# Hybrid attention trunk, one core: the sink column of the first attention, written by ScalarE instead of GpSimd

## The chip, the core and the metric

The kernel runs on one core of a Trainium2 chip. A core has five engines, each with its own in-order queue: TensorE (PE, with its weight loads shown apart as PEld), VectorE (DVE), ScalarE (ACT), GpSimd (POOL) and SyncE (SP), which here issues the DMAs. Engines wait for each other by semaphores; an instruction that waits holds up everything behind it on its own engine and nothing elsewhere. SBUF holds working tiles of 128 partitions, PSUM holds matmul results.

The metric is the device time of one launch in microseconds; lower is better. It is taken as a median of several runs.

## The reference

Two layers work on 1024 latent tokens and 256 context tokens, width 1024. Layer 0 uses windowed grouped-query attention with a sink logit per head, layer 1 a 2-D neighbourhood attention. The part that matters here is the softmax of layer 0, for the latent blocks and likewise for the context tokens:

```python
s_sink = jnp.broadcast_to(sink_l[None, :, :, None, None], s_lat.shape[:-1] + (1,))
p = jax.nn.softmax(jnp.concatenate([s_lat, s_ctx, s_sink], axis=-1), axis=-1)
p_lat = p[..., :span].astype(v.dtype)
p_ctx = p[..., span:span + C].astype(v.dtype)
```

The sink is one more logit in the sum of each row. Its probability is not used, only its share in the denominator.

## The kernel before

The program builds u (the modulated tokens, in two float32r parts, high and low, as everywhere for near-float32 matmuls), then the first attention, the output projection and layer norm of layer 0, the second attention, and the last projection with its layer norm. Names with `_A` belong to the first attention, with `_B` to the second.

The first attention is cut into 8 pairs of heads, 10 blocks of 128 queries (8 latent, 2 context) and 2 heads: 160 units, called softmaxes below. Each has a row of 640, 512 or 256 keys per query. A unit k passes through these steps:

- `qkA`: PE forms the scores S_A (L741 and L742) in PSUM.
- `sm_first`: DVE adds the mask, scales by -1/8 and takes the minimum of the row and of the negated sink in one instruction (L322), which writes s_A and, by an accumulator read, the minimum m_A. POOL copies the negated sink of the head (column of the tile `nsk`) into the column behind the row (L327). ACT takes exp(-s + m) over the row and that column and sums it into sum_A (L329, with an accumulator read).
- `sm_second`: DVE takes the reciprocal rs_A of the sum (L333), POOL scales the row by it (L334).
- `sm_transpose`: PE transposes the row by 128x128 pieces into PSUM (T_A, L341), ACT rounds it to the high part (pth_A, L345), DVE forms the low part (ptl_A, L347).
- `pvA_fn`: PE multiplies with the values (L770), ACT and DVE join the halves in `otmp` (L779, L781), POOL multiplies by the gate (L784).

s_A has three buffers, so unit k writes where unit k-3 stood; S_A and T_A share two PSUM buffers. The scores run three units ahead of the transposes.

Beside these steps PE does the projections of the gate and of the next pair's queries (pj, L212 to L214), whose weights ACT and POOL split into parts (wh L166, wl L168); the queries pass through the rotary product (L501 to L504, L696, L697). DVE, POOL and ACT also form the dot products of the layer's modulation from rows of a weight matrix loaded by DMA (gj L654, gw L655, L636), up to seven in each pair of heads.

The order on each engine is set by the framework's scheduler: it takes the program's instructions with priorities (the softmax's first part is lifted by `LIFT_A`, some others by `lift`), estimates when operands are ready, and emits one fixed queue for each engine. The proportion of projection pieces to attention steps is set by `merge`. So an edit of one instruction can move others.

Of the kernel before, what the change touches and what calls it, by code (L numbers as in the profile page):

```python
# [14 lines left out]
AF = mybir.ActivationFunctionType  # L15
# [69 lines left out]
def build(tc, i, out):  # L85
    nc = tc.nc
# [223 lines left out]
    def sm_first(pl, sc, width, bias, scale, init, name):  # L310

        s = Sub()
        s.w = width
        s.t = pl.tile([P, 641], F32, tag="s", bufs=3, name=f"s_{name}")
        s.m = pl.tile([P, 1], F32, tag="m", bufs=4, name=f"m_{name}")
        s.sum = pl.tile([P, 1], F32, tag="sum", bufs=4, name=f"sum_{name}")
        s.rs = pl.tile([P, 1], F32, tag="rs", bufs=4, name=f"rs_{name}")
        outp, in1 = s.t[:, :width], bias
        if len(bias.shape) == 3:
            outp = outp.rearrange("p (a b) -> p a b", a=bias.shape[1])  # L320
            sc = sc.rearrange("p (a b) -> p a b", a=bias.shape[1])
        nc.vector.tensor_tensor_reduce(  # L322
            outp, sc, in1, scale, init if init is not None else 3e38, ALU.add, ALU.min, accum_out=s.m
        )
        n = width
        if init is not None:
            nc.gpsimd.tensor_copy(s.t[:, width : width + 1], init)  # L327
            n += 1
        nc.scalar.activation(s.t[:, :n], s.t[:, :n], AF.Exp, bias=s.m, scale=-1.0, accum_out=s.sum)  # L329
        return s  # L330
# [400 lines left out]
    def qkA(k):  # L731
        p, b, h = subsA[k]
        q = qA[2 * p + h]
        sc = psbig(f"S_A{k}")
        ql = q[:, b * P : (b + 1) * P]
        n = len(tilesA(b)) * P - 256
        for l in range(2):
            kk = kA[p // 2, l]
            if n:
                t0 = tilesA(b)[0] * P  # L740
                mm(sc[:, 512 - n : 512], ql, kk[:, t0 : t0 + n], start=l == 0, stop=l == 1)  # L741
            mm(sc[:, 512:768], ql, kk[:, S:T], start=l == 0, stop=l == 1)  # L742
        if b == 0:
            m = msk[:, 128:640]
        elif b == 7:
            m = msk[:, 640:1152]
        elif b >= 8:
            m = msk[:, 384:640]
        else:
            m = msk[:, 0:640]  # L750
        hd = 2 * p + h
        with lift(LIFT_A):
            stA[k] = sm_first(px, sc[:, 512 - n : 768], n + 256, m, -0.125, nsk[:, hd : hd + 1], f"A{k}")
# [245 lines left out]
    bias = [bp.tile([P, 2, 640], F32, name=f"bias{n}") for n in range(2)]  # L999
# [67 lines left out]
    def qkB(k):  # L1067
        h, jp, r = subsB[k]
        j = 2 * jp + r
        sc = psbig(f"S_B{k}")  # L1070
        ql = qB[h][:, j * P : (j + 1) * P]
        t0, t1 = max(j - 1, 0) * P, min(j + 2, 8) * P
        n = t1 - t0

        ll, lc = (slice(512 - n, 512), slice(512, 768)) if j < 7 else (slice(512, 768), slice(256, 512))
        for l in range(2):
            kk = kB[h, l]
            mm(sc[:, ll], ql, kk[:, t0:t1], start=l == 0, stop=l == 1)
            mm(sc[:, lc], ql, kk[:, S:T], start=l == 0, stop=l == 1)  # L1079
        bt = bias[h % 2].rearrange("p x t -> p (x t)")  # L1080
        b0 = 0 if 0 < j < 7 else 768 if j == 0 else 384
        with lift(LIFT_B if k >= BARE_B else 0):
            stB[k] = sm_first(bp, sc[:, 512 - n : 768] if j < 7 else sc[:, 256:768], n + 256, bt[:, b0 : b0 + n + 256], -1.0, None, f"B{k}")
# [312 lines left out]
```

## Time and profile before

| what | value |
|---|---|
| median of 3 runs | 1434.78 us (1433.45 to 1435.99) |
| the profiled execution | 1434.58 us |
| its span, first to last instruction | 1432.8 us |
| first attention's softmaxes, first to last exponential | 102.9 to 572.4 us |
| ACT busy over the whole span | 51% |
| POOL busy over the whole span | 45% |

The span is what the profile's rows cover; 1.8 us of the execution lie around it. A row of grouped instructions reads: source line, engine, operation, output and input tiles with shapes, count, then busy time in us and mean duration in ns, then the idle time of the engine just before them and who ended it. A row of waits reads: who waits, for whom, us in total, times, longest. A row of the timeline reads: start, duration, engine, line, operation, and in brackets the idle time before it with its releaser.

### The profile page before, as it was taken

Reading aid. Unit: us, or ns where it says so; the run is one execution under the profiler, and the core shown is the slowest. Engines: PE = TensorE matmul, PEld = TensorE weight load, DVE = VectorE, ACT = ScalarE, POOL = GpSimd, SP = SyncE. Lnnn points to the kernel's source line nnn. Section 1 sums busy time; section 2 is a strip of 40 time slices with the busy share of each in tenths; the row PEclk is TensorE's granted clock in tenths of the full one; section 3 lists DMA queues with packets and bytes.
Section 4 is the critical chain, followed back from the end, with each engine's and each line's share of the span. In section 5 each row is a group of like instructions: output and inputs, shape, how many; then the busy total and the mean of one; then the engine's idle time right before and its main releaser. Section 6 shows DMA issues by size and latency. Waiting matters only on the chain. (4 is left out here: it accounts for less than half of the span.)

```text
span 1432.8 us, 25169 instructions
## 1 busy us (share of the span) xinstructions
PE 1390.7 (97%) x8816; PEld 1217.8 (85%) x8816; DVE 973.4 (68%) x2203; ACT 732.5 (51%) x1559; POOL 642.1 (45%) x790
## 2 busy tenths in 40 slices
PE   9999999999999999999999999999999999998996
PEld 6988898888888888888898899888988899887885
DVE  4658887878878788666433766565666565656598
ACT  4337776676776778332222545555455554557200
POOL 0326676667666666233301333333233333347583
PEclk9999999999999999999999999999999999999998
DMA  9472114123222124434287576465555564376653
GB/s 368 174 234 82 55 57 127 50 78 101 70 71 63 56 83 132 132 118 147 75 255 219 143 200 180 138 171 153 172 165 163 147 187 140 122 189 197 178 149 107
DMA packets 127597, 202.39 MB, mean 141 GB/s; under 512 B 9712, under 2 KB 65392, under 8 KB 127472
## 3 DMA queue, kind: packets, MB, share of 16 engines
q1 hardware_dynamic: 127472, 200.79, 46.6%
q8 instruction: 70, 1.15, 0.3%
q14 instruction: 55, 0.45, 0.1%
HBM read 145.18 MB, written 55.57 MB: 140 GB/s over the span
## 5 line engine op out<-in xcount | busy, mean ns | idle before, releaser
L334 POOL TENSOR_SCALAR s_B<-s_B,rs_B 128x640 f32<-128x640 f32 (+1 forms) x128 | 101.5, 793 | 285.2 <-DVE rs_B L333 249.5
L212 PE MATMUL pj<-uBh,wh 128*128 128x512 f32 (+1 forms) x448 | 175.8, 392 | 0.0
L213 PE MATMUL pj<-uBl,wh 128*128 128x512 f32 (+1 forms) x448 | 170.2, 380 | 0.0
L214 PE MATMUL pj<-uBh,wl 128*128 128x512 f32 (+1 forms) x448 | 170.0, 379 | 0.0
L329 ACT ACTIVATE s_B<-s_B,m_B 128x640 f32<-128x640 f32 (+1 forms) x128 | 102.9, 804 | 129.2 <-DVE m_B L322 129.1
L329 ACT ACTIVATE s_A<-s_A,m_A 128x641 f32<-128x641 f32 (+2 forms) x160 | 119.6, 748 | 82.8 <-DVE m_A L322 59.7
L168 POOL TENSOR_TENSOR wl<-wr,wh 128x512 fp32r<-128x512 f32 x64 | 87.0, 1360 | 162.9 <-ACT wh L166 150.0
L334 POOL TENSOR_SCALAR s_A<-s_A,rs_A 128x640 f32<-128x640 f32 (+2 forms) x160 | 129.4, 809 | 65.2 <-DVE rs_A L333 59.1
L322 DVE CUSTOM_DVE_ANT_0 s_A<-S_A,msk,nsk 128x640 f32<-128x640 f32 (+2 forms) x160 | 123.6, 774 | 32.3 <-PE S_A L742 17.2
L212 PE MATMUL pj<-uAh,wh 128*128 128x512 f32 (+1 forms) x384 | 140.1, 365 | 0.8 <-DVE otmp L781 0.8
L347 DVE TENSOR_TENSOR pt_B<-T_B,pt_B 128x640 fp32r<-128x640 f32 (+1 forms) x128 | 101.0, 789 | 55.3 <-ACT pt_B L345 54.8
L213 PE MATMUL pj<-uAl,wh 128*128 128x512 f32 (+1 forms) x384 | 137.6, 358 | 0.0
L214 PE MATMUL pj<-uAh,wl 128*128 128x512 f32 (+1 forms) x384 | 137.2, 357 | 0.0
L347 DVE TENSOR_TENSOR ptl_A<-T_A,pth_A 128x640 fp32r<-128x640 f32 (+2 forms) x160 | 114.2, 714 | 17.4 <-PE pvA L770 10.4
L341 PE MATMUL T_A<-ident,s_A 128*128 128x128 f32 x672 | 100.9, 275 | 10.5 <-DVE m_A L322 4.5
L341 PEld LDWEIGHTS T_A<-ident,s_A 128*128 128x128 f32 x672 | 77.3, 140 | 37.0 <-issue 9.9
L322 DVE CUSTOM_DVE_ANT_0 s_B<-S_B,bias 128x640 f32<-128x640 f32 (+1 forms) x128 | 100.4, 784 | 12.1 <-PE S_B L1079 10.2
L345 ACT CAST pt_B<-T_B 128x640 fp32r<-128x640 f32 (+1 forms) x128 | 84.5, 660 | 41.5 <-PE T_B L341 40.6
L345 ACT CAST pth_A<-T_A 128x640 fp32r<-128x640 f32 (+2 forms) x160 | 96.4, 602 | 17.1 <-PE T_A L341 15.7
L341 PE MATMUL T_B<-ident,s_B 128*128 128x128 f32 x608 | 88.9, 275 | 9.9 <-DVE m_B L322 4.7
L214 PEld LDWEIGHTS pj<-uBh,wl 128*128 128x128 f32 x448 | 84.3, 188 | 16.7
L341 PEld LDWEIGHTS T_B<-ident,s_B 128*128 128x128 f32 x608 | 70.6, 141 | 28.5 <-issue 12.6
(222 smaller groups left out, 3902.0 us busy)
## 6 DMA issues: line engine op xcount, KB each, us to landing
kB<-kdB SPq DMA_DIRECT2D x64, 320.0 KB, 5.0
gw<-in_wadaT SPq DMA_DIRECT2D x48, 256.0 KB, 2.8
vdB<-st SPq DMA_DIRECT2D x20, 512.0 KB, 3.4
vB<-vdB SPq DMA_DIRECT2D x16, 640.0 KB, 4.6
wada<-in_wadaC SPq DMA_DIRECT2D x16, 512.0 KB, 9.6
kdB<-st SPq DMA_DIRECT2D x16, 512.0 KB, 2.9
qdB<-st SPq DMA_DIRECT2D x16, 512.0 KB, 3.5
qB<-qdB SPq DMA_DIRECT2D x32, 256.0 KB, 4.7
```

Of the source, the lines that this page charges most:

```text
L168: e.tensor_tensor(lo, r, f32(hi), ALU.subtract)
L212: mm(pt[:, :n], hi[:, sl], rh, start=kt == 0, stop=False)
L213: mm(pt[:, :n], hi[:, sl], rl, start=False, stop=False)
L214: mm(pt[:, :n], lo[:, sl], rh, start=False, stop=kt == KT - 1)
L322: nc.vector.tensor_tensor_reduce(outp, sc, in1, scale, init if init is not None else 3e38, ALU.add, ALU.min, accum_out=s.m)
L329: nc.scalar.activation(s.t[:, :n], s.t[:, :n], AF.Exp, bias=s.m, scale=-1.0, accum_out=s.sum)
L334: nc.gpsimd.tensor_scalar(s.t[:, : s.w], s.t[:, : s.w], s.rs, 1.0, ALU.mult, ALU.mult)
L341: nc.tensor.transpose(tp[:, k * P : (k + 1) * P], s.t[:, src * P : (src + 1) * P], ident)
L345: nc.scalar.copy(pt.hi[:, :n, hl, :], tv)
L347: nc.vector.tensor_tensor(pt.lo[:, :n, hl, :], tv, f32(pt.hi[:, :n, hl, :]), ALU.subtract)
```

## The change

```diff
@@ -324,7 +324,8 @@
         )
         n = width
         if init is not None:
-            nc.gpsimd.tensor_copy(s.t[:, width : width + 1], init)
+
+            nc.scalar.activation(s.t[:, width : width + 1], s.m, AF.Identity, bias=init, scale=0.0)
             n += 1
         nc.scalar.activation(s.t[:, :n], s.t[:, :n], AF.Exp, bias=s.m, scale=-1.0, accum_out=s.sum)
         return s
```

The activation computes 0 x minimum + negated sink, so it writes the same column as the copy did. Its input is the minimum m_A of the same unit, so it can only run once DVE has that. `init` is None in the second attention, which keeps its code. Lines behind the edit carry a number one higher than before: the exponential is L329 before and L330 after.

On ACT, in the second pair of heads, the rows of four units stand like this before (s_A_n is a unit's row, pth_A and T_A its transposes, gw a dot product's second half):

```order
L329 ACTIVATE s_A_2300,sum_A_2302<-s_A_2300,m_A_2301 128x641
L636 ACTIVATE gw,dcol<-gw 128x512
L345 CAST pth_A_2327<-T_A_2329 128x5x128
L329 ACTIVATE s_A_2342,sum_A_2344<-s_A_2342,m_A_2343 128x641
L345 CAST pth_A_2327<-T_A_2362 128x5x128
L329 ACTIVATE s_A_2375,sum_A_2377<-s_A_2375,m_A_2376 128x641
L345 CAST pth_A_2395<-T_A_2397 128x5x128
L329 ACTIVATE s_A_2410,sum_A_2412<-s_A_2410,m_A_2411 128x641
```

The same place after the change:

```order
L328 ACTIVATE s_A_2300<-m_A_2301,nsk 128x1
L330 ACTIVATE s_A_2300,sum_A_2302<-s_A_2300,m_A_2301 128x641
L637 ACTIVATE gw,dcol<-gw 128x512
L346 CAST pth_A_2327<-T_A_2329 128x5x128
L328 ACTIVATE s_A_2342<-m_A_2343,nsk 128x1
L330 ACTIVATE s_A_2342,sum_A_2344<-s_A_2342,m_A_2343 128x641
L346 CAST pth_A_2327<-T_A_2362 128x5x128
L328 ACTIVATE s_A_2375<-m_A_2376,nsk 128x1
L330 ACTIVATE s_A_2375,sum_A_2377<-s_A_2375,m_A_2376 128x641
```

A 128x1 activation has come in front of each exponential, 160 in all; the exponentials and the roundings between them keep their order here.

On POOL, before, at the same units (wl and gw are products of the projections' weights and of the modulation, gA the gate):

```order
L327 COPY s_A_2300<-nsk 128x1
L168 TENSOR_TENSOR wl_2274<-wr_1879,wh_2273 128x512
L784 TENSOR_TENSOR gA_2011<-otmp,gA_2011 128x256
L334 TENSOR_SCALAR s_A_2300<-s_A_2300,rs_A_2303 128x640
L327 COPY s_A_2342<-nsk 128x1
L655 TENSOR_TENSOR gw<-gw,gh 128x512
L334 TENSOR_SCALAR s_A_2342<-s_A_2342,rs_A_2345 128x640
L327 COPY s_A_2375<-nsk 128x1
```

And after:

```order
L785 TENSOR_TENSOR gA_2011<-otmp,gA_2011 128x256
L168 TENSOR_TENSOR wl_2274<-wr_1879,wh_2273 128x512
L656 TENSOR_TENSOR gw<-gw,gh 128x512
L335 TENSOR_SCALAR s_A_2300<-s_A_2300,rs_A_2303 128x640
L335 TENSOR_SCALAR s_A_2342<-s_A_2342,rs_A_2345 128x640
L335 TENSOR_SCALAR s_A_2375<-s_A_2375,rs_A_2378 128x640
```

The copies are gone, the gate product and the modulation's product stand earlier against the scaled rows.

On DVE, before, at two of these units (ISA is the mask, scale and minimum in one, its second row the accumulator read; gj a dot product):

```order
L322 ISA s_A_2300,m_A_2301<-S_A_2295,msk,nsk 128x640
L322 ISA m_A_2301 128x1
L347 TENSOR_TENSOR ptl_A_2225<-T_A_2287,pth_A_2224 128x5x128
L283 SCALAR_TENSOR_TENSOR gA_2011<-th,pj_2_2173 128x256
L333 RECIPROCAL rs_A_2303<-sum_A_2302 128x1
L654 ISA gj,dcol<-gw,gh 128x512
L654 ISA dcol 128x1
L322 ISA s_A_2342,m_A_2343<-S_A_2337,msk,nsk 128x640
```

And after:

```order
L322 ISA s_A_2300,m_A_2301<-S_A_2295,msk,nsk 128x640
L322 ISA m_A_2301 128x1
L348 TENSOR_TENSOR ptl_A_2225<-T_A_2287,pth_A_2224 128x5x128
L283 SCALAR_TENSOR_TENSOR gA_2011<-th,pj_2_2173 128x256
L655 ISA gj,dcol<-gw,gh 128x512
L655 ISA dcol 128x1
L334 RECIPROCAL rs_A_2303<-sum_A_2302 128x1
L322 ISA s_A_2342,m_A_2343<-S_A_2337,msk,nsk 128x640
```

The dot product has moved from behind the reciprocal to ahead of it. Over the whole program a dot product stands directly behind a reciprocal rs_A 31 times before and 15 times after, directly ahead of one 9 times before and 21 times after.

## The prediction

> **What bounds the kernel now.** I read the page first: the span, the busy shares and the forty slices.
>
> ```profile
> span 1432.8 us, 25169 instructions
> PE 1390.7 (97%) x8816; PEld 1217.8 (85%) x8816; DVE 973.4 (68%) x2203; ACT 732.5 (51%) x1559; POOL 642.1 (45%) x790
> PE   9999999999999999999999999999999999998996
> ACT  4337776676776778332222545555455554557200
> PEclk9999999999999999999999999999999999999998
> ```
>
> TensorE (PE) is busy nearly all the time at a full granted clock, so the kernel's length is PE's work plus the moments in which PE stands still. The change touches only the softmax of the first attention, whose work lies in slices 3 to 16, where ScalarE (ACT) shows its sevens. So the next view is the busy time by stretch: two stretches inside the first attention, one behind it, and the whole first attention in one piece.
>
> ```profile
> core 0: us, PE busy (x) PEld busy (x) DVE busy (x) ACT busy (x) POOL busy (x), PEclk, DMA share, GB/s
> 200.00:300.00 100.00, 96.44 (x631) 84.47 (x629) 84.41 (x208) 71.32 (x165) 67.08 (x96) 1.00 0.27 83
> 300.00:400.00 100.00, 97.77 (x647) 86.09 (x645) 83.26 (x203) 69.75 (x161) 69.10 (x97) 1.00 0.26 78
> 600.00:700.00 100.00, 100.00 (x469) 82.31 (x468) 64.31 (x137) 30.13 (x53) 31.06 (x40) 1.00 0.36 116
> ...
> 100.00:585.00 485.00, 469.30 (x3057) 412.57 (x3056) 397.98 (x970) 344.52 (x779) 318.18 (x455) 1.00 0.26 81
> ```
>
> Behind the attention (600 to 700) PE has no visible idle time. Inside it, PE idles 485 - 469.3 = 15.7 us in all. VectorE (DVE) is at 398/485 = 82%, ACT at 71%, GpSimd (POOL) at 66%. So PE still leads, DVE is its nearest partner, and the change moves work from the least loaded of the three helpers to the second most loaded. What stops PE there is in the chart of waits of the same stretch:
>
> ```profile
> PE T_A L341 <- DVE m_A L322: 4.5, 6, 1.2
> PE T_A L341 <- POOL s_A L334: 4.0, 6, 0.9
> PE S_A L742 <- DVE ptl_A L347: 2.0, 7, 0.7
> PE S_A L741 <- DVE ptl_A L347: 1.3, 2, 1.1
> ...
> PE T_A L341 <- POOL s_A L327: 0.4, 1, 0.4
> PE T_A L341 <- POOL gA L784: 0.3, 1, 0.3
> ```
>
> Columns: who waits, for whom, us in total, times, longest. T_A are the transposes of the probabilities, S_A the scores. DVE ends 4.5 + 2.0 + 1.3 = 7.8 us of PE's waits, POOL 4.0 + 0.4 + 0.3 = 4.7 us, ACT none of these directly. There are 160 rows of softmax; the transposes met an unfinished POOL result in only 8 of them. ACT reaches PE by way of DVE:
>
> ```profile
> DVE rs_A L333 <- ACT s_A L329: 21.3, 45, 1.1
> DVE s_A L322 <- PE S_A L742: 17.2, 34, 2.5
> ```
>
> In 45 of 160 cases DVE stood at the reciprocal rs_A and waited for the sum from ACT's exponential. DVE runs in order, so what stood behind it waited too: the next minimum (L322) and the next low halves (ptl_A, L347), for which PE waits.
>
> **The change part by part.** *Removed from POOL*: 160 one-column copies; they also held POOL's queue.
>
> ```profile
> L327 POOL COPY s_A<-nsk 128x1 f32<-128x1 f32 x160 | 38.6, 242 | 52.8 <-PE T_A L341 49.9 <-PE pvA L770 2.3
> POOL s_A L334 <- DVE rs_A L333: 59.1, 61, 5.4
> ```
>
> That frees 160 x 0.242 = 38.6 us of POOL, and 52.8 us in which a copy stood at the head of POOL's queue until the transposes three softmaxes earlier had let go of its buffer. Neither is on PE's path by itself: POOL's own product, the scaled row, waits for DVE's rs_A in 61 cases (59.1 us), far more than PE ever waits for POOL. What the copy's lateness does cost is seen at ACT:
>
> ```profile
> ACT s_A L329 <- DVE m_A L322: 59.7, 69, 4.5
> ACT s_A L329 <- POOL s_A L334: 8.0, 8, 1.2
> ACT s_A L329 <- POOL gA L784: 5.5, 3, 1.8
> ACT s_A L329 <- POOL s_A L327: 5.0, 7, 1.4
> ACT s_A L329 <- POOL gw L655: 2.8, 3, 1.2
> ```
>
> The exponential waits for the minimum (DVE) and the copy (POOL). In 8 + 3 + 7 + 3 = 21 cases the idle time ended with POOL: 8.0 + 5.5 + 5.0 + 2.8 = 21.3 us, about 1 us each. One of them, with all three engines:
>
> ```profile
> 305.62 0.08 DVE L322 DVE_READ_ACCUMULATOR2_ANT m_A<- 128x1 f32 x1
> 304.71 1.28 POOL L655 TENSOR_TENSOR gw<-gw,gh 128x512 f32<-128x512 f32 x1
> 305.95 0.17 POOL L327 COPY s_A<-nsk 128x1 f32<-128x1 f32 x1
> 306.16 0.84 ACT L329 ACTIVATE s_A<-s_A,m_A 128x641 f32<-128x641 f32 x1 [1.41 <-POOL s_A L327]
> 306.90 0.19 ACT L329 ACTIVATION_READ_ACCUMULATOR s_A<-s_A,m_A 128x1 f32 x1
> 307.12 0.16 DVE L333 RECIPROCAL rs_A<-sum_A 128x1 f32<-128x1 f32 x1 [0.57 <-ACT s_A L329]
> ```
>
> The minimum stood at 305.70, but the copy sat behind another product of POOL until 305.95, so the exponential began at 306.16 and DVE waited 0.57 us for its sum. Note how little is won here: with the new instruction the exponential would begin at about 305.70 + 0.1 + 0.3 = 306.1. These 21.3 us of lateness go.
>
> *Added to ACT*: 160 activations on 128x1, with a bias read from a tile, each in front of its exponential and dependent on the same minimum. No row has that shape. Bounds from rows:
>
> ```profile
> L329 ACT ACTIVATE s_A<-s_A,m_A 128x641 f32<-128x641 f32 x96 | 80.0, 834 | 47.5 <-DVE m_A L322 40.8 <-POOL gw L655 2.8 <-POOL s_A L327 2.1
> L329 ACT ACTIVATE s_A<-s_A,m_A 128x257 f32<-128x257 f32 x32 | 16.4, 512 | 14.6 <-POOL s_A L334 7.2 <-DVE m_A L322 3.9 <-POOL s_A L327 2.9
> L329 ACT ACTIVATION_READ_ACCUMULATOR s_A<-s_A,m_A 128x1 f32 x160 | 30.0, 188 | 0.0
> ```
>
> Two exponentials with a tile bias give (834 - 512)/384 = 0.84 ns per column, so one column would be 512 - 256 x 0.84 = 297 ns. Below stands the 128x1 accumulator read, 188 ns; above, the 512 ns of 257 columns. I take 0.30 us, as the straight line through rows of the same kind. The exponential reads the column just written, so it starts behind the end of the new one: all 0.30 us is in series. That is 160 x 0.30 = 48 us more of ACT (bounds 30 and 82), 344.5 + 48 = 392.5 of 485, 81%. The page "ScalarE: Activation LUTs" of the Trainium skill (What ACT_TABLE_LOAD costs) gives an ACTIVATE with such a bias about 280 ns plus 0.833 ns per column, by which the addition would be an estimate of 45 us, and it adds that back-to-back ACTIVATEs overlap by about 93 ns; by that rule alone the pair would cost 30 us. The rows above show such an overlap (the exponential of 306.16 ends at 307.00, its accumulator read begins at 306.90), but between instructions that don't wait for each other; no run here shows the dependent pair.
>
> What is queued behind it: on ACT, the exponential and then the rounding of the next transposes (pth_A, L345), for which DVE's ptl_A waits; on DVE, the reciprocal.
>
> *Net lateness of the exponentials*: 48 - 21.3 = 26.7 us over 160, that is a thin 0.30 us almost everywhere and a gain of some 0.7 us in 21 places.
>
> *How much of it reaches DVE.* The 45 waits at rs_A are where nothing covers it. But the scheduler, which knows the new instruction, moves DVE work: in the built order one of the 512-wide dot products (gj) stands directly behind rs_A 31 times before and 15 times now, directly ahead of it 9 times before and 21 now. One costs
>
> ```profile
> L654 DVE CUSTOM_DVE_ANT_0 gj<-gw,gh 128x512 f32<-128x512 f32 x48 | 38.5, 802 | 0.7 <-DMA gw<-in_wadaT 0.4
> ```
>
> 0.8 us, which covers 0.30 us of lateness. So I leave 45 - 16 = 29 of 160 cases uncovered: 26.7 x 29/160 = 4.8 us more DVE idle. If that cover failed everywhere it would be 45 x 0.30 = 13.5 us.
>
> *How much of that reaches PE.* DVE has 485 - 398 = 87 us of idle time in the stage, some of it waiting for PE (17.2 us in the row above), so part of a delay is taken up there; but PE's waits for DVE show that the two follow each other closely. I take half: +2.4 us, with nothing and the whole 4.8 us as ends. The moves of DMA issues on SyncE and of a few fill matmuls on PE I cost at nothing: gj's row shows 0.4 us of waiting for its load in all, and PE's matmuls are the same ones; if that cover failed, each shifted piece could cost one more wait like the longest above, 1.2 us.
>
> *Sum*, against the profiled execution of 1434.58 us (0.2 under the median of the three runs, 1434.78): 1434.6 + 2.4 = 1437.0 us.
>
> **The rivals.**
>
> *A. POOL's queue is freed and that is what counts.* POOL without copies delivers its scaled rows and all its other products earlier; the 8 waits of PE for POOL go, while the new 0.30 us disappears under DVE's other work. It decides if the PE waits named POOL are really the copy's doing. Price: 4.7 us, 1434.6 - 4.7 = 1429.9 us. For it: 52.8 us at the head of POOL's queue. Against: of the 4.7 us only 0.4 is named for the copy itself, and PE met a late POOL product in 8 of 160 cases. The Trainium skill speaks on this side: "Perfetto Trace Analysis", Optimizing GPSIMD Operations, says "Prefer implementations on other engines where possible". The trace bears it out only in part: a 128x1 copy on POOL (242 ns) is no slower than the line puts it on ACT (297 ns).
>
> *B. All is hidden.* The transposes meet a finished row in 152 of 160 cases, gj covers the reciprocal, and the time stays: 1434.6 us.
>
> *C. ACT becomes DVE's bound.* The 45 waits at rs_A remain and grow by the full 0.30 us, the roundings pth_A come late as well, and DVE, at 82%, hands all of it to PE: 1434.6 + 13.5 = 1448.1 us. For it: ACT and DVE would both stand above 80%, with a helper's delay passed on in order. Against: 87 us of DVE idle time to absorb it. It decides from the point at which rs_A's waits grow past some 30 us.
>
> **How the numbers follow.** A measurement of this kernel can tell about 0.2%, 2.9 us, from no change. Forecast (1434.6 to 1439.4, by nothing and the whole of 4.8 us): 0.43, of which 0.20 lies under +2.9 us. A: 0.27, faster. B: 0.15, same. C: 0.15, slower. So faster 0.27, same 0.35, slower 0.38. The range goes from A's 1430 to C's 1448. The forecast's own range stands above.
>
> **What would show it right or wrong.** In the profile of the changed kernel: the new rows on ACT near 0.30 us each, ACT near 392 us in the stage, no wait of the exponential that POOL ended; rs_A's waits for ACT between 21 and 30 us (above 35, C; below 21, A or B); PE's idle time in the stage near 18 us (13 or under for A, 29 for C). Wrong altogether would be a change outside the first attention, a new row of 188 ns or of 500 ns, or transposes that begin to wait for POOL more often than before.

## The result, and the profile after

| kernel | median | runs | ratio to the kernel before, 95% interval |
|---|---|---|---|
| before | 1435.58 us (1433.45 to 1437.06) | 6 | 1 |
| after | 1440.09 us (1438.72 to 1441.07) | 6 | 1.0032 (1.0022 to 1.0042) |

The change makes the kernel 4.5 us slower. The profiled execution of after took 1441.07 us, 6.5 us more than that of before (1434.58 us); about 2 us of this difference is scatter of the two single executions, as the medians show.

The head of the page after, with the busy shares:

```profile
span 1439.3 us, 24959 instructions
...
PE 1394.8 (97%) x8816; PEld 1217.6 (85%) x8816; DVE 973.4 (68%) x2203; ACT 772.7 (54%) x1719; POOL 605.9 (42%) x630
```

ACT went up by 40.2 us and POOL down by 36.2 us; PE and DVE do the same work. The same stretches of the first attention as before, and the whole of it:

```profile
200.00:300.00 100.00, 97.18 (x626) 84.14 (x625) 84.64 (x207) 79.27 (x198) 60.93 (x64) 1.00 0.26 81
300.00:400.00 100.00, 98.42 (x652) 86.63 (x651) 83.36 (x203) 79.69 (x197) 60.62 (x63) 1.00 0.26 78
...
100.00:585.00 485.00, 468.34 (x3037) 408.92 (x3035) 394.42 (x963) 382.05 (x934) 281.69 (x296) 1.00 0.26 81
```

In the middle PE is as busy as before or a little busier (98.42 against 97.77), with ACT at 79% in place of 70%. So the loss isn't spread over the attention. It sits at its two ends, here of before:

```profile
100.00:200.00 100.00, 95.53 (x620) 84.13 (x619) 80.84 (x195) 69.98 (x156) 66.36 (x93) 1.00 0.27 85
...
500.00:585.00 85.00, 81.54 (x527) 71.41 (x528) 70.49 (x172) 63.65 (x140) 50.97 (x76) 1.00 0.32 99
```

and of after:

```profile
100.00:200.00 100.00, 93.84 (x606) 82.25 (x605) 78.08 (x191) 76.40 (x186) 55.75 (x59) 1.00 0.28 86
...
500.00:585.00 85.00, 80.60 (x523) 69.66 (x521) 69.32 (x171) 68.68 (x166) 46.30 (x49) 1.00 0.31 94
```

PE's busy time falls by 1.7 and 0.9 us there, and its matmuls by 14 and 4. The groups of the widest exponential (641 columns, 96 of the 160) and of the new instruction:

```profile
L330 ACT ACTIVATE s_A<-s_A,m_A 128x641 f32<-128x641 f32 x96 | 79.9, 833 | 2.3
...
L328 ACT ACTIVATE s_A<-m_A,nsk 128x1 f32<-128x1 f32 x160 | 46.9, 293 | 53.9 <-DVE m_A L322 52.2 <-DVE rs_A L334 0.4
```

The wait for the minimum, 59.7 us in front of the exponential before, now stands in front of the small activation, and the widest exponentials themselves wait 2.3 us in place of 47.5. One softmax in the timeline (start, duration):

```profile
305.16 0.62 ACT L166 CAST wh<-wr 128x512 fp32r<-128x512 f32 x1 [0.79 <-PE pj L213]
...
305.33 0.08 DVE L322 DVE_READ_ACCUMULATOR2_ANT m_A<- 128x1 f32 x1
...
305.69 0.29 ACT L328 ACTIVATE s_A<-m_A,nsk 128x1 f32<-128x1 f32 x1
...
306.01 0.83 ACT L330 ACTIVATE s_A<-s_A,m_A 128x641 f32<-128x641 f32 x1
...
306.75 0.18 ACT L330 ACTIVATION_READ_ACCUMULATOR s_A<-s_A,m_A 128x1 f32 x1
...
306.97 0.16 DVE L334 RECIPROCAL rs_A<-sum_A 128x1 f32<-128x1 f32 x1 [0.95 <-ACT s_A L330]
```

The exponential starts 0.03 us behind the end of the small activation (305.69 + 0.29): the whole 0.29 us is in series. It is so in 122 of the 160 softmaxes; in the other 38 the new order has put another ACT instruction between the two, most often a copy of the output (otmp, 13) or half of a dot product (gw, 7), or a rounding of transposes (pth_A, 7). In the softmax shown the minimum stood at 305.41, and the activation began when ScalarE's cast of weights was about to end (305.78). The waits of the stage:

```profile
DVE rs_A L334 <- ACT s_A L330: 31.9, 50, 1.1
DVE s_A L322 <- PE S_A L743: 25.5, 48, 2.5
...
PE T_A L342 <- DVE m_A L322: 5.4, 7, 1.6
...
PE T_A L342 <- POOL s_A L335: 2.1, 4, 1.1
```

DVE's waits at the reciprocal grew from 21.3 to 31.9 us; PE's waits for POOL's scaled rows fell from 4.0 to 2.1.

To see where lateness arises I also took from each trace the start of the first transpose of every softmax (0 to 159, 20 for each pair of heads) and subtracted the start in before. After's softmax 27, in the second pair, is 2.4 us late; 134, in the seventh, 2.9; 159, the last, 5.3. Over 107 softmaxes in the middle it loses 0.5 us, and as much as 2.4 us over the last 25. The built order of PE differs most in just these places. Around the transposes of softmax 147, in the last pair, it reads, before (rows of the built program without their numbers; pj38 is the last gate projection):

```
L341 MATMUL T_A147<-ident,s_A147 128x128 x5
L212 MATMUL pj38_2<-uAh2,wh38 128x256
L741 MATMUL S_A150<-kA3_0,qA14 128x384
L742 MATMUL S_A150<-kA3_0,qA14 128x256
L741 MATMUL S_A150<-kA3_1,qA14 128x384
L742 MATMUL S_A150<-kA3_1,qA14 128x256
L213 MATMUL pj38_2<-uAl2,wh38 128x256
```

and now:

```
L212 MATMUL pj38_2<-uAh2,wh38 128x256
L342 MATMUL T_A147<-ident,s_A147 128x128 x5
L213 MATMUL pj38_2<-uAl2,wh38 128x256
L742 MATMUL S_A150<-kA3_0,qA14 128x384
L743 MATMUL S_A150<-kA3_0,qA14 128x256
L742 MATMUL S_A150<-kA3_1,qA14 128x384
L743 MATMUL S_A150<-kA3_1,qA14 128x256
```

Pieces of projection have moved ahead of the transposes and the scores. So there are two candidates for the loss: the **price** of the instruction in series, and the **order** that the scheduler made of the new program.

### The profile page after: what moved, and what is told of

It is laid out like the page before. It is cut to its first block, busy times and chain, and to the rows that moved or that the text cites. A ratio compares the mean times of both kernels' runs of the same rounds, so it can differ in the third digit from the quotient of the medians.

```text
span 1439.3 us, 24959 instructions
## 1 busy us (share of the span) xinstructions
PE 1394.8 (97%) x8816; PEld 1217.6 (85%) x8816; DVE 973.4 (68%) x2203; ACT 772.7 (54%) x1719; POOL 605.9 (42%) x630
## 5 line engine op out<-in xcount | busy, mean ns | idle before, releaser
L335 POOL TENSOR_SCALAR s_A<-s_A,rs_A 128x640 f32<-128x640 f32 (+2 forms) x160 | 119.4, 747 | 137.3 <-DVE rs_A L334 107.6
L330 ACT ACTIVATE s_B<-s_B,m_B 128x640 f32<-128x640 f32 (+1 forms) x128 | 102.9, 804 | 130.5 <-DVE m_B L322 130.5
L330 ACT ACTIVATE s_A<-s_A,m_A 128x641 f32<-128x641 f32 (+2 forms) x160 | 119.6, 747 | 4.1
L342 PE MATMUL T_A<-ident,s_A 128*128 128x128 f32 x672 | 101.1, 275 | 10.6 <-DVE m_A L322 5.4
L214 PEld LDWEIGHTS pj<-uBh,wl 128*128 128x128 f32 x448 | 84.3, 188 | 16.7
```

Of the source, the lines that this page charges most:

```text
L214: mm(pt[:, :n], lo[:, sl], rh, start=False, stop=kt == KT - 1)
L335: nc.gpsimd.tensor_scalar(s.t[:, : s.w], s.t[:, : s.w], s.rs, 1.0, ALU.mult, ALU.mult)
L342: nc.tensor.transpose(tp[:, k * P : (k + 1) * P], s.t[:, src * P : (src + 1) * P], ident)
```

## The experiments

To tell them apart, the order of each engine can be held fixed: the program is built as it stands, and each instruction then gets an ordering edge, without a semaphore, to the one that is to stand in front of it on its engine. "Old order" is the order of the kernel before, "new order" that of the changed kernel. The edges add no instruction: x1 below has 24959, as the changed kernel, and x2 has 25169, as the kernel before. No run pins the kernel before to its own order, so what pinning costs by itself is not shown.

```diff
+def pin(tc):
+    by = {i.name: i for i in tc.nc.cur_bb.bb.instructions}
...
+        for a, b in zip(seq, seq[1:]):
+            tc.add_manual_dep(by[f"I-{b}"], f"I-{a}", how, reason="order")
...
         build(tc, ins, o)
+        pin(tc)
```

All twelve kernels were timed in five rounds against the kernel before. The second column tells whether the order was pinned; lateness is that of the profiled execution at softmax 27, 134 and 159, in us against before. It comes from one execution each, so it carries their scatter: w4, in the old order, was 2.2 us late at its very first transposes.

| run | order | column written by | median us | ratio (95%) | lateness at 27, 134, 159 |
|---|---|---|---|---|---|
| x1 | old | activation on the minimum | 1446.38 | 1.0077 (1.0063 to 1.0090) | 1.5, 9.2, 12.1 |
| x2 | new | GpSimd's copy | 1437.73 | 1.0017 (1.0008 to 1.0026) | 0.7, -0.4, 1.7 |
| x3 | old | two activations on the minimum | 1476.75 | 1.0288 (1.0274 to 1.0302) | 6.8, 34.1, 41.8 |
| x4 | old | activation on the sink alone | 1437.38 | 1.0013 (1.0004 to 1.0022) | -0.4, 1.6, 3.0 |
| y1 | new in the middle only | activation on the minimum | 1442.49 | 1.0051 (1.0038 to 1.0065) | 4.0, 4.5, 7.4 |
| y4 | old | nothing | 1433.48 | 0.9989 (0.9980 to 0.9997) | -1.2, -2.1, -2.2 |
| z4 | free | activation on the sink alone | 1435.46 | 1.0008 (1.0000 to 1.0017) | -1.5, -1.0, 0.8 |
| z3 | free | two activations on the minimum | 1446.67 | 1.0080 (1.0066 to 1.0093) | 1.8, 6.7, 12.9 |
| w1 | old, 56 reciprocals later | activation on the minimum | 1450.34 | 1.0101 (1.0087 to 1.0115) | 2.7, 9.4, 14.2 |
| w2 | new at the ends only | GpSimd's copy | 1438.68 | 1.0017 (1.0008 to 1.0026) | 0.3, 0.1, 2.7 |
| w3 | old | activation, sink as both operands | 1440.41 | 1.0031 (1.0019 to 1.0042) | 0.1, 3.1, 5.1 |
| w4 | old | activation on the minimum, no bias | 1441.15 | 1.0035 (1.0022 to 1.0049) | 2.8, 7.1, 8.9 |

The kernel before had a median of 1435.35 us beside x1 to x4, 1434.98 beside y1 to z3, and 1435.82 beside w1 to w4. Costs below are ratios times 1435 us.

### The instruction in the old order, and the old instruction in the new order

x1 is the changed kernel with the order of before; x2 is the kernel before with the order of the changed kernel (GpSimd's copies stand where the scheduler put them).

> The activation on the minimum, directly in front of its exponential, but every engine keeps the order it has in the kernel before (PE, VectorE and SyncE rows identical; GpSimd without its 160 copies; ScalarE with the 160 small activations added). Theory of the price (0.29 us in series per softmax reaches TensorE): the same loss as the changed kernel, 1439 to 1441 us. Theory of the order (the loss sits in the first and the last pair of heads, where the scheduler has put TensorE's pieces in another order): at most 1 us above the kernel before, 1434 to 1437 us. Theory that the freed GpSimd is worth something by itself: below 1434 us.

> GpSimd's copy as before, but TensorE, VectorE and SyncE in the order of the changed kernel, and ScalarE too without the small activation. Theory of the order: it keeps most of the loss, 1438 to 1441 us. Theory of the price: it is as fast as the kernel before, 1434 to 1437 us. If price and order only cost together, both this run and the one with the new instruction in the old order lie at 1434 to 1437 us.

In x1 every exponential stands directly behind its small activation, and starts 0.03 us after its end. x1 cost 11.0 us, more than the price theory had for it and far more than the changed kernel's 4.6; x2 cost 2.4 us. So neither theory holds alone. The price is large, the new order costs something by itself, and together they cost less than the price alone: with the new instruction the new order **saves** 11.0 - 4.6 = 6.4 us. The waits of x1 show the price arriving at DVE and then at PE:

```profile
DVE rs_A L333 <- ACT s_A L329: 46.2, 87, 1.3
...
PEld T_A L341 <- POOL s_A L334: 13.5, 22, 1.4
...
PE T_A L341 <- DVE m_A L322: 5.9, 10, 1.2
...
PE T_A L341 <- POOL s_A L334: 3.7, 9, 0.9
...
PE S_A L741 <- DVE ptl_A L347: 2.8, 6, 0.9
...
PE S_A L742 <- DVE ptl_A L347: 2.3, 7, 0.8
PE T_A L341 <- DVE ptl_A L347: 2.1, 3, 0.9
```

The weight loads of the transposes (PEld, which overlaps PE) had these waits for POOL before:

```profile
PEld T_A L341 <- POOL s_A L334: 9.5, 17, 1.4
...
PEld T_A L341 <- POOL s_A L327: 5.1, 5, 1.3
```

The wait at the reciprocal is 46.2 us in 87 cases, against 21.3 in 45 before. PE meets it by way of DVE: its waits for the minimum and for ptl_A add up to 5.9 + 2.8 + 2.3 + 2.1 = 13.1 us, against 7.8 before. Its waits for POOL's scaled rows hardly moved: 3.7 us against 4.0, and 13.5 at the weight loads, against 9.5 and the 5.1 that were put down to the copy. The lateness grows evenly through the middle pairs, by 7.7 us from softmax 27 to 134, where the changed kernel grows by 0.5. In x2, without the new instruction, DVE waits at the reciprocal about as before:

```profile
DVE rs_A L333 <- ACT s_A L329: 19.8, 44, 1.1
```

### More and less of the price

x3 writes the column twice; z3 below does the same with a free order:

```diff
-nc.scalar.activation(s.t[:, width : width + 1], s.m, AF.Identity, bias=init, scale=0.0)
+[nc.scalar.activation(s.t[:, width : width + 1], s.m, AF.Identity, bias=init, scale=0.0) for _ in range(2)]
```

In x4 (and, with a free order, z4) the activation reads the sink and not the minimum, so it can run while DVE still searches the minimum:

```diff
-nc.scalar.activation(s.t[:, width : width + 1], s.m, AF.Identity, bias=init, scale=0.0)
+nc.scalar.activation(s.t[:, width : width + 1], init, AF.Identity)
```

> Order of the kernel before on all engines, with two identical small activations in front of each exponential, so 0.58 us in series in place of 0.29, and ScalarE some 430 us busy of 485. Theory of the price: twice the loss of the changed kernel, +9 us on the kernel before, 1443 to 1446 us. Theory of the order: ScalarE still has slack, under 3 us above the kernel before, 1435 to 1438 us.

> Order of the kernel before; the column is written by a ScalarE activation of the sink alone (no operand from the minimum), directly in front of the exponential, so that ScalarE can run it while VectorE still works on the minimum. ScalarE's added busy time is the same, some 40 us, but it is out of the chain from minimum to exponential wherever ScalarE is idle there. If the series part of the price costs anything, this lies below the kernel with the activation on the minimum in the same order, by up to the whole loss; if only ScalarE's occupancy costs, the two are equal within 1 us.

x3 cost 41 us where the price theory had 9: not twice, but nearly four times the 11 us of x1. The second 0.29 us per softmax costs 30 us of 47, so nearly two thirds of it reach the end, while of the first about a quarter did. The stage of x3 shows it:

```profile
100.00:585.00 485.00, 446.28 (x2822) 379.89 (x2822) 368.69 (x903) 399.08 (x1019) 269.10 (x278) 1.00 0.24 73
```

ACT is still idle for 86 of 485 us there, so it isn't ACT's total load that binds; PE idles 39 us. What binds is the chain minimum, small activation, exponential, reciprocal, scaled row, transposes. x4 agrees: as an activation out of that chain it cost 1.9 us in place of 11.

Two things differ between x1 and x4, though: the place in the chain, and the length (294 against 201 ns, since x4 reads no bias from a tile). w3 keeps the long form and leaves the chain; w4 keeps the chain with the short form, and leaves the sink's value out of the column (it writes 0 times the minimum). w3:

```diff
-nc.scalar.activation(s.t[:, width : width + 1], s.m, AF.Identity, bias=init, scale=0.0)
+nc.scalar.activation(s.t[:, width : width + 1], init, AF.Identity, bias=init, scale=0.0)
```

and w4:

```diff
-nc.scalar.activation(s.t[:, width : width + 1], s.m, AF.Identity, bias=init, scale=0.0)
+nc.scalar.activation(s.t[:, width : width + 1], s.m, AF.Identity, scale=0.0)
```

> Order of the kernel before; the same form of activation (a bias from a pointer, 293 ns in the changed kernel) with the sink as both operands, so that it doesn't wait for the minimum. The independent activation without a bias from a pointer took 201 ns and cost 2.0 us, the one on the minimum 294 ns and 11 us. Theory that the place in series decides: 1436 to 1439 us. Theory that the longer form on ScalarE decides: 1443 to 1447 us.

> Order of the kernel before; an activation on the minimum without the sink as bias (it writes 0 times the minimum into the column, so the sink's value is left out), some 200 ns in place of 294, still in series between minimum and exponential. Theory that the series time decides, steeper than in proportion (0.29 us gave 11 us, 0.59 us gave 41 us): 0.20 us gives 4 to 7.5 us, 1439 to 1442.5 us. Theory that a second semaphore wait between VectorE and ScalarE costs, whatever the length: 1444 to 1448 us.

The four forms in their groups, x1 first:

```profile
L327 ACT ACTIVATE s_A<-m_A,nsk 128x1 f32<-128x1 f32 x160 | 47.0, 294 | 65.9 <-DVE m_A L322 65.2
```

w4:

```profile
L327 ACT ACTIVATE s_A<-m_A 128x1 f32<-128x1 f32 x160 | 32.3, 202 | 68.9 <-DVE m_A L322 68.2
```

w3:

```profile
L327 ACT ACTIVATE s_A<-nsk 128x1 f32<-128x1 f32 x160 | 46.8, 293 | 0.6
```

x4:

```profile
L327 ACT ACTIVATE s_A<-nsk 128x1 f32<-128x1 f32 x160 | 32.1, 201 | 0.6
```

| in the old order | 0.20 us long | 0.29 us long |
|---|---|---|
| on the minimum | 5.0 us (w4) | 11.0 us (x1) |
| on the sink alone | 1.9 us (x4) | 4.4 us (w3) |

w4 came out within its theory's 4 to 7.5 us, without a sign of an extra cost for the wait itself. w3 (1440.41 us) lay between both theories: out of the chain the long form still costs 4.4 us. It runs free only where ACT stands idle in front of the exponential; where ACT comes from other work, it is in series all the same. In its timeline the activation follows the cast of weights at once and pushes the exponential, whose minimum has stood since 304.17:

```profile
303.88 0.62 ACT L166 CAST wh<-wr 128x512 fp32r<-128x512 f32 x1 [0.82 <-PE pj L213]
...
304.08 0.09 DVE L322 DVE_READ_ACCUMULATOR2_ANT m_A<- 128x1 f32 x1
...
304.40 0.29 ACT L327 ACTIVATE s_A<-nsk 128x1 f32<-128x1 f32 x1
...
304.72 0.84 ACT L329 ACTIVATE s_A<-s_A,m_A 128x641 f32<-128x641 f32 x1
```

### What the freed GpSimd is worth

y4 leaves the sink column out of the softmax (no copy, no activation, the exponential one column shorter), in the old order. What remains is POOL without its 160 copies.

```diff
-nc.gpsimd.tensor_copy(s.t[:, width : width + 1], init)
-n += 1
+pass
```

> The sink column is left out of the softmax altogether (no copy, no activation, the exponential one column shorter), with every engine in the order of the kernel before: what remains is the effect of GpSimd's freed queue alone. Theory that freeing GpSimd is worth something: 1425 to 1431 us. Theory that GpSimd's copy lies beside other work and costs nothing: 1433 to 1436 us, as the kernel before.

It is 1.6 us faster, interval 0.4 to 2.9: little, and inside the 1433 to 1436 us of the theory that the copy costs nothing. That is about all that any way to write the column can win in this order. DVE's waits at the reciprocal fell a little, since the exponentials no longer wait for late copies:

```profile
DVE rs_A L333 <- ACT s_A L329: 17.3, 40, 1.0
```

### Where the new order costs, and where it saves

y1 has the activation on the minimum, with the new order for softmaxes 27 to 134 and the old one in front of and behind them. w2 has GpSimd's copy, with the new order at the ends and the old one in the middle.

> The activation on the minimum. All engines follow the changed kernel's order for softmaxes 27 to 134 of the 160 (middle pairs of heads) and the order of the kernel before in front of and behind them. With the activation, the old order everywhere cost 11 us and the new order everywhere 4.5 us. Theory that the new order of VectorE and ScalarE in the middle pairs is what takes in the price: 1439 to 1442 us (TensorE's stalls in the middle pairs as in the changed kernel, 29 us, not 34). Theory that the gain of the new order is made in the first and the last pair: 1443 to 1447 us.

> GpSimd's copy as before; the order of the changed kernel only in front of softmax 27 and behind softmax 134, the order of the kernel before between. Theory that the new order of TensorE in the first and the last pair costs by itself: 1436.5 to 1439 us, as the new order everywhere (+2.4 us). Theory that it costs in the middle: 1434 to 1436 us.

w2 cost 2.4 us, the same as x2 with the new order everywhere: the order of the ends costs by itself, without the new instruction. Its lateness arises behind softmax 134 (0.1 to 2.7 us), and the last stretch of the stage shows PE's loss:

```profile
500.00:585.00 85.00, 79.20 (x516) 68.95 (x516) 68.82 (x167) 62.27 (x138) 49.65 (x75) 1.00 0.31 99
```

PE is busy 79.2 us there against 81.5 before, though the program has the same instructions. The order of every engine is exchanged there, so it isn't shown that PE's moved pieces are what costs. y1 cost 7.3 us, just above what the theory of the middle had. Its lateness explains the rest: from softmax 27 to 134 it grows by 0.5 us, as in the changed kernel, against 7.7 us in x1; but 2.8 us arise between softmaxes 20 and 27, where the two orders are joined, against 0.6 in x1 and 1.0 in the changed kernel. So the new order of the middle pairs takes in nearly all of the price there. The order at the ends gives nothing back that could be seen. At the far end it doesn't seem to cost anything either, once the new instruction is in: over the last 25 softmaxes the activation on the minimum loses 2.9 us in the old order (x1, y1) and 2.4 in the new one (the changed kernel), and the new order with GpSimd's copy 2.1 and 2.6 (x2, w2). By these single executions either alone makes a loss of this size, and the two don't add up.

w1 asks whether it is DVE's order: the old order, but 56 of the 160 reciprocals stand later, behind the next minimum or a piece of side work. The expectation below says that the changed kernel has them so; VectorE's rows bear that out in part only. All 20 dot products that w1 lets pass a reciprocal pass it there too. But 36 reciprocals have come to stand behind the next minimum in w1, and 18 of these stand ahead of it in the changed kernel. One of the 18, in VectorE's rows (w1 against the old order):

```diff
-L333 RECIPROCAL rs_A22<-sum_A22 128x1
 L322 ISA s_A23,m_A23<-S_A23,msk,nsk 128x640
 L322 ISA m_A23 128x1
+L333 RECIPROCAL rs_A22<-sum_A22 128x1
```

> The activation on the minimum in the order of the kernel before, as in the run that cost 11 us, with one thing changed: 56 of the 160 reciprocals stand one to some places later in VectorE's queue, behind the next minimum or another piece of work, as the changed kernel has them; no other engine's order differs. Theory that the loss comes from VectorE waiting at the reciprocal with work queued behind it: 1440 to 1444 us, and VectorE's waits at the reciprocal fall from 46 us to 30 to 40. Theory that the order of ScalarE (casts against exponentials) is what takes in the price: 1444.5 to 1448 us, as without the move.

It fell outside of both theories: 1450.34 us, 3.4 us slower than x1. The waits:

```profile
DVE s_A L322 <- PE S_A L742: 36.4, 51, 2.5
...
DVE rs_A L333 <- ACT s_A L329: 21.2, 39, 1.2
...
PEld T_A L341 <- POOL s_A L334: 16.9, 19, 1.4
...
PE T_A L341 <- POOL s_A L334: 7.2, 8, 0.9
```

The wait at the reciprocal fell as expected and further, from 46.2 to 21.2 us, the value of before, and nothing was won. A later reciprocal makes the scaled row later; PE waits more for it (16.9 + 7.2 us against 13.5 + 3.7), its scores come later, and DVE waits for those instead (36.4 us; 18.0 in x1). So a shorter wait at the reciprocal doesn't by itself mean less lost time: moving only the reciprocal moves the wait around the loop. Since 18 reciprocals stand behind a minimum that the changed kernel doesn't put ahead of them, and minima wait for PE, w1 doesn't settle whether VectorE's real new order would take in the price by itself. (The waits come from one execution with a mean granted clock of 0.945, and are not shown at 0.995; the time is: three others of the kernel, at that clock, took 1449.20 to 1450.78 us.) In the changed kernel ScalarE's and VectorE's side work has moved together: over softmaxes 27 to 134, a dot product now stands ahead of a reciprocal that it stood behind 16 times, a sum of the output (otmp) 7 times; on ACT an output copy or half of a dot product now stands ahead of an exponential that it stood behind 14 times. Which of these moves takes in the price wasn't separated: no run takes one engine's order from the changed kernel and the others' from before.

### Free orders

> The column written by a ScalarE activation of the sink alone, without the operand from the minimum, and the scheduler left to order all engines. In the old order this cost 2.0 us. If ScalarE's occupancy is what is left of the price, 1436 to 1439 us; if the scheduler puts it where ScalarE is idle, 1434 to 1436 us; if it moves TensorE's order in the first and last pair as it did with the activation on the minimum, 1437 to 1440 us.

> Two identical activations on the minimum in front of each exponential, the scheduler left to order all engines; in the old order the pair cost 41 us. Theory that a rearranged order takes in the series part as long as ScalarE has slack (some 430 us busy of 485): 1444 to 1455 us, far below the 1476.75 us of the old order. Theory that ScalarE's place in the loop decides whatever the order: 1465 to 1480 us.

z4, the activation on the sink alone with the scheduler free, is the best that was found for ScalarE: 1435.46 us, level with the kernel before (1.0000 to 1.0017) and 3.4 us under the changed kernel by the ratios. There the scheduler has put other work of ACT between the activation and its exponential in all 160 softmaxes, so the column is written ahead of the chain. z3 cost 11.5 us where the same two activations cost 41 in the old order: the scheduler takes in about 30 of 41 us, as it takes in 6.4 of 11 with one. No kernel that computes the full softmax beat the kernel before, and by y4 there are some 1.6 us to win in the order of before.

## Why the prediction was right, and where it wasn't

The forecast was 1437.0 us in a range of 1430 to 1448; the kernel took 1440.09. The sign and the range held; the steps behind them held in part:

1. **Removed from POOL, no part of PE's path: nearly right.** y4 puts the freed queue at 1.6 us, not nothing. The 21.3 us of exponentials that POOL's lateness held up did go: no wait of the exponential ends with POOL any more. Rival A had 4.7 us for this and no price: a third of it is there. In y4 PE's own waits that end with POOL did fall from 4.7 to 0.3 us, but 3.1 us of waits of the transposes for ptl_A came in their place. The count of 8 late POOL results took in PE's own rows alone; the weight loads of the same transposes stood for a scaled row or the copy in 17 + 5 = 22 more. The rule that spoke for A (the Trainium skill, "Perfetto Trace Analysis", Optimizing GPSIMD Operations) isn't borne out: none of the kernels that write the column on ScalarE was faster than before.

2. **The new instruction at 0.30 us, all in series: right for the most part.** 293 ns, and in 122 of 160 softmaxes the exponential follows 0.03 us behind its end; in the other 38 other work of ACT stands between them. The Trainium skill, "ScalarE: Activation LUTs" (What ACT_TABLE_LOAD costs), has 280 ns plus 0.833 per column for a bias by pointer and 93 ns less without one; the runs show 293 and 201 to 202 ns and agree to within 15 ns. Its overlap of back-to-back activations doesn't shorten the pair, since they depend on each other. ACT's busy time in the stage rose to 382 us, not to 392. Over the whole program it rose by 40.2 us where the new instructions add up to 46.9: the start of the small activation can overlap the end of an unrelated instruction ahead of it, as with the cast in the timeline above (0.09 us).

3. **Net lateness 26.7 us, of which 29/160 uncovered, 4.8 us at DVE: mis-sized.** DVE's waits at the reciprocal grew by 10.6 us. Without the reordering they grew by 24.9 (x1), so nearly the whole net lateness reached DVE. The bound "if that cover failed everywhere", 13.5 us of waiting, was too low as well: it let the 45 waits grow, but in x1 there are 87. As a bound on lost time, which is how rival C used it, it held (x1 lost 11.0). That the cover came from a changed order was right. The reason given, a dot product that no longer stands behind the reciprocal, was not tested alone: w1 moves 20 dot products so and loses more, but it also holds 18 reciprocals behind a minimum where the changed kernel doesn't.

4. **Half of it reaches PE, +2.4 us: right in size by luck.** The price inside the order that was built is the changed kernel against x2: 1.0032 - 1.0017 = 0.15%, 2.1 us (about 0.2 to 4.1, from the two intervals taken together). Between the same two kernels DVE's waits at the reciprocal grew by 12.1 us, from 19.8 to 31.9. So about a sixth of a wait 2.5 times as large reached PE; too small a wait and too large a share made up for each other. In the old order the share was near the half: 11.0 of 24.9.

5. **"The moves of DMA issues on SyncE and of a few fill matmuls on PE I cost at nothing": this step failed.** x2 and w2 price the changed order alone at 2.4 us, in the last pair of heads for the most part. The cover that I named, "PE's matmuls are the same ones", says nothing of when they come: pieces of the projection moved ahead of transposes and scores that others wait for. That these pieces make the loss is likely, but no run moved them alone. With this term the sum would have been 1434.6 + 2.4 + 2.4 = 1439.4 us, or 1440.4 on the median of 1435.58 beside the changed kernel. That is one way to split the loss: the order first, then the instruction. The other way gives 11.0 us for the instruction and -6.4 for the order, so neither is a term that can be carried to another sum.

So the mechanism of the forecast, a delay in series that reaches PE by way of DVE and is covered in part by a new order, was right; its sizes were not, and the total hides two larger numbers of opposite sign. Of the rivals, C (ScalarE's lateness handed on in full, 1448.1 us; from some 30 us at the reciprocal) is what the instruction does in the old order: 46.2 us of waits and 1446.4 us. The scheduler's new order kept the changed kernel out of it, with 31.9 us just past the point that I had set. B (hidden, 1434.6) is what the activation becomes when it doesn't read the minimum and the order is free (z4). Of the signs that were named, PE's idle time in the stage was 16.7 us and no 18, between the forecast and A: in a stretch of fixed length the lateness shows as fewer matmuls (3037 against 3057) more than as idle time, so this was a poor measure.

## What to carry to other kernels

An instruction is priced by its place in the loop's chain, not by its engine's spare time: with ScalarE idle for over 20% of the stage, 0.29 us in series cost 11 us over 160 softmaxes in a fixed order; a second 0.29 us cost 30 us more, with ScalarE still idle for 18%; and much the same instruction off the chain cost 2 to 4 us. GpSimd's copy, which sits beside the chain, cost 1.6 us: it was in the right place. Where a scheduler orders the program, each edit is two changes, the instruction and the order, and what they cost need not add up: hold the order fixed and exchange one at a time before explaining a difference of a few tenths of a per cent.

## What the runs showed of the hardware that was not expected

- Cost against series time is bent: 0.20, 0.29 and 0.59 us in front of each exponential gave 5.0, 11.0 and 41 us in the same order.
- A wait can be moved without winning anything: DVE's wait for ACT fell from 46.2 to 21.2 us in w1, and its wait for PE rose from 18.0 to 36.4 us (one execution, at a lower granted clock than x1's).
